# A two-layer hybrid backbone: softmax attention in two batches a group, retention scores by head pairs

## The chip, the cores and the metric

The kernel runs on one core of one Trainium2 chip. The metric is the device time of one execution in microseconds; what is shown is the median of the runs. The profile is that of one execution.

## The reference

Two post-norm layers act on 384 tokens of width 1024: 128 context tokens (block 0) and 256 latent tokens (blocks 1 and 2). All arithmetic is float32. A layer is a token mixer followed by a squared-ReLU MLP; both are modulated by a conditioning vector, and each ends in a layer norm. What matters here is the mixer:

```
p = h @ w_in                      # columns: q/kv latents, B's q k v g, C's q k v, D's q k v, four gates
A: latent attention, 4 heads      # dense; latent tokens also see 128 cached keys
B: retention, 4 heads             # (q k^T * decay) v, from both ends, plus a carried state
C: windowed attention, 4 q heads on 2 kv heads, a sink logit per head
D: dense attention, 4 q heads on 2 kv heads, q and k RMS-normalised
softmax: m = max(s); e = exp(s - m); p = e / sum(e) (+ exp(sink - m) for C)
retention_out: per head (o - mean) * rsqrt(var + eps) * gain * silu(gate)
y = sum_i sigmoid(gate_i) * (o_i @ w_branch_i); y = y @ w_o
x = layernorm(alpha * x + g1 * y);  f = square(relu(h @ w_up)) @ w_down;  x = layernorm(alpha * x + g2 * f)
```

Context tokens attend to the 128 context keys alone; a latent block attends to 256 latent keys and 128 cached ones, so its scores are 384 wide and those of the context block 128.

## The kernel before, in words

Every large product is made of three matmuls (`mm3`, L119 to L122): both operands are split into a high and a low float32r part, and high*high, low*high and high*low are added up in one PSUM bank. Each weight tile is loaded by a queue of SP, its high part is cast by ScalarE (L281) and its low part subtracted by VectorE (L125, `split_low`). `Stream` (L238) keeps four loads and two splits ahead.

The mixer of a layer goes in two stretches. First the input projection: chunks of 256 columns (L1068), each for the three token blocks `t` in turn (`proj`, L613): 8 steps of k, three matmuls each with 256 columns moving, into a bank of `psg`, then ScalarE moves it to a `t2` tile `tm[key, t]` (L588). Keys are "a", "c", "d", "b1" (the retention's q and k) and "b2" (its v and g). Layer 0 makes "c" and "a" beforehand; layer 1 has two chunks more. Then the four branches' gates and products (L1127), in the order A, C, D, B: `gates` (L1083) makes two gate tiles of 24 matmuls with 384 columns, `products` (L1094) multiplies the branch's output with its weights in two `psa` banks, and VectorE and GpSimd add them up (L1111 to L1117).

Between these groups of matmuls, `tick` (L461) calls `Pipe.step` (L425): it starts one more task of a list written by hand (L1037 to L1065) and calls the next stage of each task under way, oldest first. `held` keeps the instructions of a step behind what had been issued two steps before (`HOLD`); beyond that, the framework orders instructions of an engine by readiness and order of writing. After 22 ticks each tick also issues two or three steps of `ada_vector` (L346): VectorE operations over 1024 columns that make the modulation vectors of later stages (L370). These, and the scratch they write, share `t2` with the rest. Ahead of the last branch the list is run dry (L1131), the attention's memory is given back, and that of the second half (`p2`) is taken.

A task of softmax attention (`attend`, L621) is one group `g` (two heads `j`) and one token block `u`. Its stages are `scores` (L630: two banks of `psa`, one matmul for each head, mask, maximum, exponential with its sum on ScalarE, reciprocal and scaling on VectorE), `turn` (L665: transposes of p into two `psm` banks, copied to `pT` by ScalarE for j = 0 and by VectorE for j = 1) and `values` (L678). There are six of them for each branch, in the order u = 1, 2, 0 for each group. The retention's tasks are `prep_b` (L898: four transposes of q and k for each block), `states_b` (L909; its decayed k is made by GpSimd, L915), `scores_bp` (L937), `scores_b` (L948, one for each head) and `out_b` (L973). In C, D and B a head has 64 channels, so that the two heads of a pair lie in the lower and upper 64 partitions.

`out_product` (L1255) is the product that ends each half of a layer. Its last four steps of k are made block by block, with the layer norm of one block beside the matmuls of the next: `raw` (L1175), `stats` (L1185), `normalise` (L1194), `turn` (L1202), `high` and `low` into `hT`, and `update` on GpSimd. In the first half, the products of the first three MLP tiles run in between (`first_up`, L1415), with `square_u` (L1386) and `turn_u` (L1392); their squares are taken by VectorE (L1389), those of the other tiles by ScalarE (L1437). At the end of layer 1, the last block's second half is made in two pieces of 256 columns (L1308), and `end` (L1243) writes the result.

Pools that matter: `t2` has 12 tiles of 128x512 (`T2N`), `p` and `pT` two each (`PN`), `psa` three banks, `psm` and `psg` two, `pso` one.

Of the kernel before, what the change touches and what calls it, by code (L numbers as in the profile page):

```python
# [28 lines left out]
T2N = 12  # L29
# [64 lines left out]
def kernel(ctx, tc, a):  # L94
# [360 lines left out]
    for l in range(L):  # L455
# [165 lines left out]
        def attend(i, q_of, k_of, v_of, scale, sink=None, mask=None):  # L621
            ob = {}

            def batch(g, u):
                nb = 3 if u else 1
                nk = nb * P
                keys = slice(P, 512) if u else slice(0, P)
                st_ = {}

                def scores():  # L630
                    mx, neg, su = small([P, 2], "mx"), small([P, 2], "neg"), small([P, 2], "su")
# [7 lines left out]
                    for j in range(2):  # L639
                        s = ss[j]  # L640
                        if mask is not None and u:
                            c0 = P if u == 1 else 0
                            nc.vector.tensor_tensor(out=s[:, c0:c0 + P], in0=s[:, c0:c0 + P], in1=mask[u - 1], op=ALU.add)
                        nc.vector.reduce_max(mx[:, j:j + 1], s[:, :nk], axis=AX.X)
                    if sink is not None:
                        sk = sink[:, 2 * g:2 * g + 2]
                        nc.vector.scalar_tensor_tensor(out=mx, in0=mx, scalar=scale, in1=sk, op0=ALU.mult, op1=ALU.max)
                        nc.vector.tensor_scalar(out=neg, in0=mx, scalar1=-1.0, scalar2=None, op0=ALU.mult)
                        es = small([P, 2], "es")
# [3 lines left out]
                    for j in range(2):  # L653
                        nc.scalar.activation(p[:, j, :nk], ss[j][:, :nk], AF.Exp, bias=neg[:, j:j + 1], scale=scale,
                                             accum_out=su[:, j:j + 1])
# [4 lines left out]
                    for j in range(2):  # L660
                        nc.vector.tensor_scalar(out=p[:, j, :nk], in0=p[:, j, :nk], scalar1=su[:, j:j + 1], scalar2=None,
                                                op0=ALU.mult)
                    st_["p"] = p

                def turn():  # L665
                    p = st_["p"]
                    pT = at.tile([P, 2, NTOK], F32, tag="pT", name=nm("pT"), bufs=PN)
                    for j in range(2):
                        tb = bank(psm)
                        for b in range(nb):  # L670
                            nc.tensor.transpose(tb[:, b * P:(b + 1) * P], p[:, j, b * P:(b + 1) * P], ident)
                        if j == 0:
                            nc.scalar.copy(pT[:, j, :nk], tb[:, :nk])
                        else:
                            nc.vector.tensor_copy(pT[:, j, :nk], tb[:, :nk])
                    st_["pT"] = pT

                def values():  # L678
                    pT = st_["pT"]
                    if u == 1:  # L680
                        ob[g] = bank(pso)
                    if u == 1 and g == 0:
                        new_o(i)
                    for b in range(nb):
                        blk = b + 1 if u else 0
                        for j in range(2):
                            mm(ob[g][64 * j:64 * j + 64, u * P:(u + 1) * P], lhsT=v_of(g, j, blk),
                               rhs=pT[:, j, b * P:(b + 1) * P], start=(b == 0), stop=(b == nb - 1))
                    if u == 0:
# [7 lines left out]
            return [batch(g, u) for g in range(2) for u in (1, 2, 0)]  # L697
# [85 lines left out]
        def keys_a():  # L783
            for i in range(2):
                kb = bank(psa)
                for j in range(2):
                    h = 2 * i + j
                    mm(kb[64 * j:64 * j + 64, :], lhsT=w_uk[:, h * 64:(h + 1) * 64], rhs=ckvT, start=True, stop=True)
# [109 lines left out]
        def prep_b(t):  # L898
            def turn():
                if t == 0:  # L900
                    bt["qk"] = at.tile([P, 4, NTOK], F32, tag="k6", name=nm("qkB"), bufs=2)
                x = tm["b1", t]
                tb = bank(psm)
                for i in range(4):
                    nc.tensor.transpose(tb[:, i * P:(i + 1) * P], x[:, i * P:(i + 1) * P], ident)
                nc.scalar.copy(bt["qk"][:, :, t * P:(t + 1) * P], tb.rearrange("p (i n) -> p i n", i=4))
            return (turn,)

        def states_b():  # L909
            kds = []  # L910

            def dec():
                for d in range(2):
                    kd = t2("kd")
                    nc.gpsimd.tensor_tensor(  # L915
                        out=kd[:, 0:256].rearrange("p (h d) -> p h d", h=4),
                        in0=tm["b1", 0][:, 256:512].rearrange("p (h d) -> p h d", h=4),
                        in1=bt["dcol"][:, 4 + d].unsqueeze(2).to_broadcast([P, 4, 64]), op=ALU.mult)
                    kds.append(kd)

# [16 lines left out]
        def scores_bp():  # L937
            qk, dtab = bt["qk"], bt["dtab"]
            attp = bt["attp"] = t2("attp").rearrange("p (h n) -> p h n", h=4)
            for j in range(2):  # L940
                r = slice(64 * j, 64 * j + 64)
                pb = bank(psa)
                for i in range(2):
                    mm(pb[:, i * P:(i + 1) * P], lhsT=qk[r, 2 + i, 0:P], rhs=qk[r, i, 0:P], start=True, stop=True)
                nc.vector.tensor_tensor(out=attp[:, j::2], in0=pb[:, 0:256].rearrange("p (i n) -> p i n", i=2),
                                        in1=dtab[:, j::2, 1], op=ALU.mult)

        def scores_b(h):  # L948
            def f():
                qk, dtab = bt["qk"], bt["dtab"]  # L950
                i, j = divmod(h, 2)
                r = slice(64 * j, 64 * j + 64)
                pb = bank(psa)
                att = bt["att", h] = t2("atts").rearrange("p (b n) -> p b n", b=2)
                for jb in range(2):
                    mm(pb[:, jb * 256:(jb + 1) * 256], lhsT=qk[r, 2 + i, (1 + jb) * P:(2 + jb) * P], rhs=qk[r, i, P:NTOK],
                       start=True, stop=True)
                for jb in range(2):
                    nc.vector.tensor_tensor(
                        out=att[:, jb], in0=pb[:, jb * 256:(jb + 1) * 256],  # L960
                        in1=dtab[:, h, 1 - jb:3 - jb].rearrange("p a n -> p (a n)"), op=ALU.mult)
# [95 lines left out]
        for t in range(3):  # L1057
            pipe.add(*prep_b(t))
        pipe.add(*states_b())
        pipe.add(scores_bp)  # L1060
        for h in range(4):
            pipe.add(*scores_b(h))
# [5 lines left out]
        chunks = [("d", 0, None), ("d", 256, None), ("b1", 0, None), ("b1", 256, 0.125), ("b2", 0, None), ("b2", 256, 0.5)]  # L1068
# [577 lines left out]
```

## Time and profile before

| | |
|---|---|
| median of 3 runs | 1299.65 us (1298.49 to 1302.27) |
| the profiled execution | 1298.03 us |
| its span, first to last instruction | 1296.2 us |
| matmul instructions | 7362 |
| TensorE busy | 1269.4 us |
| mean granted TensorE clock | 0.996 of full speed |

The span is cut into stretches by the work that is done in them: the start with the first inputs up to 54.5 us; the mixer of layer 0 to about 345 us and its end and first layer norm to 402 us; the MLP to 680 us, with the second layer norm at its end; the mixer of layer 1 to about 975 us; its MLP to the end. A float32 matmul or score stands in the profile as two instructions, a transpose as one. Start times of neighbouring matmuls tell what each costs TensorE; their durations overlap.

### The profile page before, as it was taken

The numbers are of one execution on the slowest core, as the hardware profiler recorded it, in microseconds if no ns is written. First come the engines' busy times: TensorE is split into PE (matmuls) and PEld (weight loads), VectorE is DVE, ScalarE is ACT, GpSimd is POOL, SyncE is SP. The second block draws the span as 40 slices with busy tenths as digits, with TensorE's granted clock in tenths as the row PEclk, the third lists the DMA queues.
The fourth block names the chain that finished last, engine by engine and source line by source line (L and its number), as shares of the span: only waits on it lengthen the run. The fifth ranks groups of instructions, "written<-read, shape, count | busy, mean of one in ns | idle before, by whom it ended". The sixth has DMA issues, their size and how long they took to land. (4 is left out here: it accounts for less than half of the span.)

```text
span 1296.2 us, 19421 instructions
## 1 busy us (share of the span) xinstructions
PE 1269.4 (98%) x7362; PEld 1142.7 (88%) x7362; DVE 877.9 (68%) x1629; ACT 566.9 (44%) x1031; POOL 199.0 (15%) x218
## 2 busy tenths in 40 slices
PE   8999999999999999999999999999999999999996
PEld 6788888999988999999898888899998899999995
DVE  4655899996669999543485689967455993333336
ACT  4554445323535444444365445423343644444441
POOL 0010301323223000000061120012321500000003
PEclk9999999999999999999999999999999999999999
DMA  9833254665535888554323224543644263334421
GB/s 369 305 106 97 99 172 157 208 228 210 179 114 188 264 271 275 172 166 147 114 75 120 91 90 163 190 169 117 227 157 152 91 219 130 130 130 151 164 76 49
DMA packets 64686, 211.68 MB, mean 163 GB/s; under 512 B 9233, under 2 KB 13265, under 8 KB 64465
## 3 DMA queue, kind: packets, MB, share of 16 engines
q1 hardware_dynamic: 61872, 201.49, 45.1%
q0 software_dynamic: 2432, 8.42, 1.9%
q8 instruction: 58, 0.95, 0.3%
q10 hardware_dynamic: 288, 0.52, 0.1%
q14 instruction: 36, 0.29, 0.1%
HBM read 206.28 MB, written 4.13 MB: 162 GB/s over the span
## 5 line engine op out<-in xcount | busy, mean ns | idle before, releaser
L125 DVE TENSOR_TENSOR wl<-raw,wh 128x1024 fp32r<-128x1024 f32 x250 | 318.5, 1278 | 286.2 <-ACT wh L281 278.4
L281 ACT CAST wh<-raw 128x1024 fp32r<-128x1024 f32 x250 | 261.7, 1051 | 455.0 <-PE bank L121 297.4
L120 PE MATMUL bank<-hTh,wh 128*128 128x384 f32 x976 | 330.2, 338 | 0.3
L122 PE MATMUL bank<-hTh,wl 128*128 128x384 f32 x976 | 327.5, 336 | 0.0
L121 PE MATMUL bank<-hTl,wh 128*128 128x384 f32 x976 | 327.3, 335 | 0.0
L120 PEld LDWEIGHTS bank<-hTh,wh 128*128 128x128 f32 x976 | 183.3, 188 | 7.3 <-issue 2.9
L121 PEld LDWEIGHTS bank<-hTl,wh 128*128 128x128 f32 x976 | 183.3, 188 | 2.4 <-issue 0.3
L122 PEld LDWEIGHTS bank<-hTh,wl 128*128 128x128 f32 x976 | 183.2, 188 | 0.6 <-issue 0.3
L121 PE MATMUL bank<-wl,uh 128*128 128x512 f32 (+1 forms) x388 | 151.1, 389 | 0.0
L122 PE MATMUL bank<-wh,ul 128*128 128x512 f32 (+1 forms) x388 | 150.9, 390 | 0.0
L120 PE MATMUL bank<-wh,uh 128*128 128x512 f32 (+1 forms) x388 | 150.3, 387 | 0.0
L370 DVE CUSTOM_DVE_ANT_0 acc<-raw,csr,bT 128x1024 bf16<-128x1024 f32 x80 | 103.7, 1320 | 0.0
L120 PE MATMUL bank<-wh,hTh 128*128 128x256 f32 x336 | 99.9, 297 | 2.3 <-ACT tmc L594 2.3
L370 DVE CUSTOM_DVE_ANT_0 acc<-lnc,csr,bT 128x1024 bf16<-128x1024 f32 x80 | 99.6, 1280 | 0.0
L1117 POOL TENSOR_TENSOR tt<-tt,tt 128x384 f32<-128x384 f32 x48 | 61.6, 1303 | 240.6 <-DVE tt L1116 234.0
L121 PE MATMUL bank<-wl,hTh 128*128 128x256 f32 x336 | 95.4, 284 | 0.0
L122 PE MATMUL bank<-wh,hTl 128*128 128x256 f32 x336 | 95.4, 284 | 0.0
L122 PEld LDWEIGHTS bank<-wh,ul 128*128 128x128 f32 x388 | 72.8, 188 | 14.9
L121 PEld LDWEIGHTS bank<-wl,uh 128*128 128x128 f32 x388 | 72.8, 188 | 13.8
L120 PEld LDWEIGHTS bank<-wh,uh 128*128 128x128 f32 x388 | 72.9, 188 | 13.6
L120 PEld LDWEIGHTS bank<-wh,hTh 128*128 128x128 f32 x336 | 64.0, 190 | 6.3 <-ACT tmc L594 2.6
L121 PEld LDWEIGHTS bank<-wl,hTh 128*128 128x128 f32 x336 | 64.2, 191 | 2.5 <-issue 1.6
(263 smaller groups left out, 1810.2 us busy)
## 6 DMA issues: line engine op xcount, KB each, us to landing
raw<-in_w_g_dram SPq DMA_DIRECT2D x64, 512.0 KB, 3.7
raw<-in_w_d_dram SPq DMA_DIRECT2D x64, 512.0 KB, 3.5
raw<-in_w_u_dram SPq DMA_DIRECT2D x58, 512.0 KB, 3.8
raw<-in_w_av_dram SPq DMA_DIRECT2D x40, 512.0 KB, 3.4
lnc<-in_w_av_dram SPq DMA_DIRECT2D x40, 512.0 KB, 4.4
raw<-in_w_q_dram SPq DMA_DIRECT2D x28, 512.0 KB, 4.6
raw<-in_w_ada_dram SPq DMA_DIRECT2D x16, 512.0 KB, 8.5
raw<-in_w_b_dram SPq DMA_DIRECT2D x16, 512.0 KB, 3.7
```

The source lines that it names most:

```text
L120: mm(out, lhsT=a_hl[0], rhs=b_hl[0], start=start, stop=False)
L121: mm(out, lhsT=a_hl[0], rhs=b_hl[1], start=False, stop=False)
L122: mm(out, lhsT=a_hl[1], rhs=b_hl[0], start=False, stop=stop)
L125: nc.vector.tensor_tensor(out=low, in0=x, in1=high.bitcast(F32), op=ALU.subtract)
L281: nc.scalar.copy(wh, raw)
L370: nc.vector.tensor_tensor_reduce(out=alloc().bitcast(BF16), in0=w, in1=csr[:, c], scale=1.0, scalar=bT[:, l, u, b:b + 1], op0=ALU.mult, op ...
L1117: nc.gpsimd.tensor_tensor(out=acc[c], in0=acc[c], in1=t_, op=ALU.add)
```

## The change

- `Pipe.step` calls the stages of one step in two rounds: first all that are not marked late, then those marked late. Late are the transposes of the softmax (`turn`) and the new first stage of `states_b`.
- `attend` makes two tasks of a group in place of three: blocks 1 and 0 together (384 and 128 columns side by side in one bank for each head), and block 2. The score matmuls of the two heads stand next to each other for each block. `p` and `pT` are 512 wide. The group's output is moved after block 2.
- The retention's q and k are no longer projected by token and then transposed: the chunks "b1" become "qk", made by channels (`qk_b`: weights stationary, 384 tokens moving), four groups of 24 matmuls in place of six, each with one tick. `prep_b` goes. `states_b` transposes k of block 0 back (two transposes), and VectorE, not GpSimd, multiplies it with the decay. The new tile has a tag of its own ("kb").
- `scores_b` takes two heads at once, with their matmuls next to each other in two banks; `scores_bp` likewise.
- `keys_a` makes one matmul of 128 columns in place of two of 64.
- In the layer norm ScalarE normalises the last block's second half too, and the last block of all is no longer cut into pieces of 256 columns. `square_u` squares on ScalarE.
- `T2N` is 10 in place of 12, and the scratch for dynamic DMA 4096 in place of 8192.

```diff
     def step(self):
...
-            for t in list(self.live):
-                if t:
-                    with held(marks):
-                        t.pop(0)()
-                if not t:
-                    self.live.remove(t)
+            stages = [t.pop(0) for t in self.live if t]
+            for late in (False, True):
+                for f in stages:
+                    if getattr(f, "late", False) == late:
+                        with held(marks):
+                            f()
+            self.live = [t for t in self.live if t]
...
                 def scores():
...
-                    p = at.tile([P, 2, NTOK], F32, tag="p", name=nm("p"), bufs=PN)
-                    ss = []
-                    for j in range(2):
-                        s = bank(psa)
-                        mm(s[:, :nk], lhsT=q_of(g, j, slice(u * P, (u + 1) * P)), rhs=k_of(g, j, keys),
-                           start=True, stop=True)
-                        ss.append(s)
+                    p = at.tile([P, 2, 512], F32, tag="p", name=nm("p"), bufs=PN)
+                    ss = [bank(psa) for _ in range(2)]
+                    for u, nb, c in segs:
+                        for j in range(2):
+                            mm(ss[j][:, c], lhsT=q_of(g, j, slice(u * P, (u + 1) * P)),
+                               rhs=k_of(g, j, slice(P, 512) if u else slice(0, P)), start=True, stop=True)
...
+                turn.late = True
...
-            return [batch(g, u) for g in range(2) for u in (1, 2, 0)]
+            return [batch(g, us) for g in range(2) for us in ((1, 0), (2,))]
...
-        def prep_b(t):
...
+        def qk_b(i0, scale):
+
+            def f(w, i):
+                if i0 + i == 0:
+                    bt["qk"] = at.tile([P, 4, NTOK], F32, tag="kb", name=nm("qkB"))
+                b = bank(psg)
+                for k in range(KT):
+                    mm3(b[:, :NTOK], tuple(q[:, i * P:(i + 1) * P] for q in w[k]), hk(k), k == 0, k == KT - 1)
+                if scale is None:
+                    nc.scalar.copy(bt["qk"][:, i0 + i, :], b[:, :NTOK])
+                else:
+                    nc.scalar.mul(bt["qk"][:, i0 + i, :], b[:, :NTOK], scale)
+            return f
...
             def dec():
+                tb = bank(psm)
+                for i in range(2):
+                    nc.tensor.transpose(tb[:, i * P:(i + 1) * P], bt["qk"][:, 2 + i, 0:P], ident)
                 for d in range(2):
                     kd = t2("kd")
-                    nc.gpsimd.tensor_tensor(
+                    nc.vector.tensor_tensor(
...
-        def scores_b(h):
+        def scores_b(i):
+
             def f():
                 qk, dtab = bt["qk"], bt["dtab"]
...
+                pbs = [bank(psa) for _ in range(2)]
                 for jb in range(2):
...
+                    for j in range(2):
+                        r = slice(64 * j, 64 * j + 64)
+                        mm(pbs[j][:, jb * 256:(jb + 1) * 256], lhsT=qk[r, 2 + i, (1 + jb) * P:(2 + jb) * P],
+                           rhs=qk[r, i, P:NTOK], start=True, stop=True)
...
-        chunks = [("d", 0, None), ("d", 256, None), ("b1", 0, None), ("b1", 256, 0.125), ("b2", 0, None), ("b2", 256, 0.5)]
+        chunks = [("d", 0, None), ("d", 256, None), ("qk", 0, None), ("qk", 2, 0.125), ("b2", 0, None), ("b2", 256, 0.5)]
...
             def normalise():
                 for h in range(2):
-                    if t == 2 and h == 1:
-                        nc.vector.tensor_scalar(out=z[h], in0=src[h], scalar1=mv[:, 0:1], scalar2=rs[:, 1:2],
-                                                op0=ALU.subtract, op1=ALU.mult)
-                    else:
-                        nc.scalar.activation(z[h], src[h], AF.Identity, bias=rs[:, 3:4], scale=rs[:, 1:2])
+                    nc.scalar.activation(z[h], src[h], AF.Identity, bias=rs[:, 3:4], scale=rs[:, 1:2])
...
-                    cuts = (0, 512, 768, 1024)
-                    last_part(2, None, cuts)
-                    sums(2, None, cuts)
+                    last_part(2)
+                    sums(2)
...
-            nc.vector.tensor_tensor(out=r, in0=r, in1=r, op=ALU.mult)
+            nc.scalar.activation(r, r, AF.Square)
```

## Rows read from the trace of the kernel before

**Rows 1.** The page's first part: busy time and instructions of each engine.

```profile
PE 1269.4 (98%) x7362; PEld 1142.7 (88%) x7362; DVE 877.9 (68%) x1629; ACT 566.9 (44%) x1031; POOL 199.0 (15%) x218
```

**Rows 2.** Busy time by stretch: its length, then PE, PEld, DVE, ACT, POOL (instructions).

```profile
80.00:330.00 250.00, 245.95 (x1601) 223.84 (x1600) 205.68 (x463) 104.32 (x231) 50.61 (x46) 1.00 0.49 163
...
205.00:285.00 80.00, 79.90 (x483) 73.01 (x483) 79.38 (x133) 29.20 (x56) 21.69 (x15) 1.00 0.63 206
...
820.00:960.00 140.00, 140.00 (x837) 135.34 (x837) 92.85 (x183) 47.85 (x78) 31.45 (x30) 1.00 0.48 169
```

**Rows 3.** What TensorE waited for: us in total, times, longest.

```profile
PE bank L671 <- DVE p L661: 3.1, 5, 1.2
PE bank L1395 <- DVE r L1389: 2.3, 4, 0.7
PE bank L120 <- ACT tmc L594: 2.3, 1, 2.3
...
PE bank L1027 <- DVE oB L1019: 1.9, 1, 1.9
```

**Rows 4.** Timeline of TensorE (start, us): first and last of nine 256-column, eight 384-column matmuls.

```profile
60.80 0.28 PE L120 MATMUL bank<-wh,hTh 128*128 128x256 f32 x1
...
61.76 0.28 PE L122 MATMUL bank<-wh,hTl 128*128 128x256 f32 x1
...
215.01 0.33 PE L120 MATMUL bank<-hTh,wh 128*128 128x384 f32 x1
...
216.23 0.33 PE L121 MATMUL bank<-hTl,wh 128*128 128x384 f32 x1
```

**Rows 5.** The same: the retention's transposes of one block, and the matmul behind them.

```profile
233.52 0.60 PE L905 MATMUL bank<-ident,tmb 128*128 128x128 f32 x4
233.87 0.42 PE L121 MATMUL bank<-hTl,wh 128*128 128x384 f32 x1
```

**Rows 6.** The same: the retention's scores of one head, and the matmul behind them.

```profile
261.53 1.13 PE L956 MATMUL bank<-qkB 64*128 64x256 f32 x4
262.59 0.44 PE L120 MATMUL bank<-o,wh 128*128 128x384 f32 x1
```

**Rows 7.** The same: scores of two heads next to each other, and of one alone.

```profile
128.82 0.92 PE L636 MATMUL bank<-qk 64*128 64x384 f32 x4
...
163.99 0.91 PE L636 MATMUL bank<-qk 64*128 64x384 f32 x2
```

**Rows 8.** The same: values of a context block by themselves, and the matmul behind them.

```profile
117.58 0.44 PE L687 MATMUL bank<-pT,va 128*64 128x128 f32 x4
117.95 0.38 PE L120 MATMUL bank<-wh,hTh 128*128 128x256 f32 x1
```

**Rows 9.** Squares of 128x384 on VectorE and ScalarE, normalising on ScalarE: groups of the span.

```profile
L1389 DVE TENSOR_TENSOR r<-r 128x384 f32<-128x384 f32 x6 | 7.7, 1287 | 0.0
...
L1437 ACT ACTIVATE r<-r 128x384 f32<-128x384 f32 x58 | 30.5, 526 | 1.7
...
L1200 ACT ACTIVATE z<-z,lnrs 128x512 f32<-128x512 f32 x15 | 11.6, 811 | 26.9 <-POOL lnrs L1192 26.9
```

**Rows 10.** Timeline of VectorE at the end: two 512-column operations, the first and last 256-column ones.

```profile
1280.55 0.70 DVE L1179 SCALAR_TENSOR_TENSOR bank<-x,bank 128x512 f32<-128x512 f32 x1
...
1281.28 0.70 DVE L1182 BATCH_NORM_STATS2 lnst<-bank 128x6 f32<-128x512 f32 x1
...
1285.40 0.43 DVE L1178 TENSOR_TENSOR bank<-bank,lnc 128x256 f32<-128x256 f32 x1 [0.65 <-PE bank L122]
...
1288.27 0.26 DVE L1186 BATCH_NORM_AGGREGATE lnmv<-lnst 128x2 f32<-128x24 f32 x1
```

**Rows 11.** Groups of VectorE in the stretch of 205 to 285 us.

```profile
L370 DVE CUSTOM_DVE_ANT_0 acc<-raw,csr,bT 128x1024 bf16<-128x1024 f32 x33 | 44.0, 1365 | 0.0
```

**Rows 12.** Groups of VectorE in the span: copies of transposed p, and decay on 256 columns.

```profile
L675 DVE COPY pT<-bank 128x384 f32<-128x384 f32 x24 | 13.3, 555 | 8.4 <-PE bank L671 8.4
...
L945 DVE TENSOR_TENSOR attp<-bank,dtab 128x256 f32<-128x256 f32 x4 | 1.5, 412 | 0.0
```

More of the change, by code (lines that the diff above doesn't have):

```diff
@@ L28 @@
 T1N = 11
-T2N = 12
+T2N = 10
 PN = 2
@@ new lines, in scores @@
+                    for i, (u, nb, c) in enumerate(segs):
+                        for j in range(2):
+                            s = ss[j][:, c]
+                            if mask is not None and u:
+                                c0 = P if u == 1 else 0
+                                nc.vector.tensor_tensor(out=s[:, c0:c0 + P], in0=s[:, c0:c0 + P], in1=mask[u - 1],
+                                                        op=ALU.add)
+                            nc.vector.reduce_max(mx[:, i, j:j + 1], s, axis=AX.X)
@@ L785, in keys_a @@
                 kb = bank(psa)
-                for j in range(2):
-                    h = 2 * i + j
-                    mm(kb[64 * j:64 * j + 64, :], lhsT=w_uk[:, h * 64:(h + 1) * 64], rhs=ckvT, start=True, stop=True)
+                mm(kb, lhsT=w_uk[:, i * P:(i + 1) * P], rhs=ckvT, start=True, stop=True)
                 nc.scalar.copy(kTA[0:64, 2 * i, :], kb[0:64, :])
@@ L949, in f @@
             def f():
                 qk, dtab = bt["qk"], bt["dtab"]
[L951 to L954, printed above, removed]
+                pbs = [bank(psa) for _ in range(2)]
                 for jb in range(2):
-                    mm(pb[:, jb * 256:(jb + 1) * 256], lhsT=qk[r, 2 + i, (1 + jb) * P:(2 + jb) * P], rhs=qk[r, i, P:NTOK],
-                       start=True, stop=True)
@@ L958, in f @@
[L958 to L961, printed above, removed]
+                    for j in range(2):
+                        r = slice(64 * j, 64 * j + 64)
+                        mm(pbs[j][:, jb * 256:(jb + 1) * 256], lhsT=qk[r, 2 + i, (1 + jb) * P:(2 + jb) * P],
+                           rhs=qk[r, i, P:NTOK], start=True, stop=True)
@@ L1056 @@
             pipe.add(*b)
-        for t in range(3):
-            pipe.add(*prep_b(t))
         pipe.add(*states_b())
         pipe.add(scores_bp)
-        for h in range(4):
-            pipe.add(*scores_b(h))
+        for i in range(2):
+            pipe.add(*scores_b(i))
         for t in (1, 2, 0):
@@ L1076 @@
         for key, c0, scale in chunks:
-            proj(by_k([stream.next(), stream.next()], 4), 256, evac_to(key, c0, scale), tick)
+            w = by_k([stream.next(), stream.next()], 4)
+            if key == "qk":
+                for i in range(2):
+                    qk_b(c0, scale)(w, i)
+                    tick()
+            else:
+                proj(w, 256, evac_to(key, c0, scale), tick)
         acc = [None] * KT
@@ L1165, in layer_norm @@
             gb, lg_, lb_ = consts[cnd], consts[2], consts[3]
-            width = 256 if mod is None and t == 2 else 512
-            st = p2.tile([P, 4, 6], F32, tag="lnst", name=nm("lnst"), bufs=2)
+            st = p2.tile([P, 2, 6], F32, tag="lnst", name=nm("lnst"), bufs=2)
             mv = p2.tile([P, 2], F32, tag="lnmv", name=nm("lnmv"), bufs=2)
@@ L1180, in raw @@
                                                op0=ALU.mult, op1=ALU.add)
-                for i in range(c.start, c.stop, width):
-                    nc.vector.bn_stats(st[:, len(groups)], src[h][:, i:i + width])
-                    groups.append(i)
+                nc.vector.bn_stats(st[:, h], src[h][:, c])
             def stats():
-                nc.vector.bn_aggr(mv, st[:, 0:len(groups)])
+                nc.vector.bn_aggr(mv, st)
                 nc.vector.tensor_scalar(out=rs[:, 0:1], in0=mv[:, 1:2], scalar1=EPS, scalar2=None, op0=ALU.add)
```

93 lines of the change are left out of this document (45 added, 48 removed).

## The prediction

> **What bounds the kernel now.** I read the busy times first: TensorE is busy for 1269.4 of 1296.2 us, VectorE for 68%, ScalarE 44%, GpSimd 15% [rows 1]. A busy TensorE may still be stretched, so next come the stretches: in layer 0's mixer it is busy for 245.95 of 250 us, and over 205 to 285 us for 79.90 of 80 [rows 2]. What it waits for by name is little: 3.1 us for the scaled p ahead of the softmax's transposes, 2.3 us for squares, 2.3 us for an evacuation at the start of the projection, 1.9 us for the last retention output [rows 3]. So the span is the sum of what TensorE is given to do, and an instruction less on it, or a pause less between two kinds of its work, is time gained, as long as the other engines keep up. Whether they do is the second thing to see: over 205 to 285 us VectorE is busy for 79.38 of 80 us [rows 2], 44.0 of them in operations for later modulation vectors [rows 11]. Two engines are full at once there. In the mixer of layer 1 VectorE has room: 92.85 of 140 us over 820 to 960 [rows 2].
>
> The sum goes by start times. Nine matmuls of 256 columns start over 0.96 us, so one takes 0.120; eight of 384 start over 1.22 us, so one takes 0.174 [rows 4].
>
> **The change, part by part.** Terms are for both layers; minus is time gained.
>
> q and k by channels: a layer's 144 matmuls of 0.120 us (17.3 us) become 96 of 0.174 (16.7): -0.6, twice, **-1.2 us**. Columns are the same; only the fixed part of a matmul falls away. The new evacuation by ScalarE is hidden by its idle 56% [rows 1]; if ScalarE were late, the two `psg` banks would hold up the next group.
>
> No transposes of q and k: six visits (three blocks, two layers) of 0.35 us, from 233.52 to 233.87, and the matmul behind each is 0.42 long, not 0.33: 0.09 more of restart [rows 4, 5]. 6 x 0.44 = 2.6. Added are two visits with half as many transposes, 0.18 + 0.09 each: 0.5. **-2.1 us**. The decayed k moves to VectorE: four operations on 256 columns of 0.412 [rows 12], 1.6 us, hidden unless VectorE is full; then it counts in the last term.
>
> Retention scores: a head takes 1.06 us (261.53 to 262.59) and a restart of 0.10 (0.44 against 0.34) [rows 6]. That two heads side by side cost what one costs shows in the softmax's scores: four instructions for two heads 0.92 us, two for one head alone 0.91 [rows 7]. Eight visits become four of the same length: 4 x 1.16, **-4.6 us**. Bounds: 0 if the heads aren't issued in pairs and the visits stay, 4.6 if all are.
>
> Softmax heads of C and D: most pairs are already side by side, but I find three pairs of 384 columns and two of 128 issued apart in the trace, one of them at 163.99 us [rows 7]. Written next to each other, they would save some 0.94 and 0.5 each, 3.9 in all; nothing forces it, since readiness orders them, and more pairs could also come apart. Between +3.9 and -3.9, and nearer to the gain, since both banks are now taken first: half of it, **-1.9 us**.
>
> 36 batches become 24: twelve times a context block's scores and values join those of another block. Values by themselves take 0.37 us and a restart of 0.10 (0.38 against 0.28) [rows 4, 8]. Sure is only the restart, 24 x 0.10, **-2.4 us**; above, 24 x 0.37 = 8.9; below 0.
>
> Transposes last: the p they read has a score visit more of time. Of the 3.1 us of waits [rows 3] I take half: **-1.5 us**. Late next would be the copies of the transposed p, see the rivals.
>
> The list is run dry ahead of the last branch. In layer 0 there are 18 + 24 ticks and 42 tasks, the last of four stages, so three steps run with no matmul group between them; the 1.9 us wait for the retention output [rows 3] is there. Now 31 tasks meet 16 + 24 ticks: **-1.9 us**.
>
> Squares of the first tiles: VectorE takes 1287 ns for each, ScalarE 526 for the same shape [rows 9], and TensorE waited 2.3 us for them [rows 3]: **-2.3 us**; below, 0 if ScalarE is busy there. The Trainium skill ("ScalarE: Activation LUTs", Rules for kernel authors) says the opposite for this operation: multiply on VectorE, not on ScalarE; by that rule the sum would lack these 2.3 us. Here the rows disagree with it, and I go by them; what speaks for it is a rival.
>
> Normalising on ScalarE (0.811 us [rows 9]) stands one behind the other there, and VectorE is free earlier to give back the bank that the next transposes want: taken as 0, between +0.8 and -0.8 for each of three norms.
>
> The end: VectorE starts the last two pieces at 1285.40, when TensorE has left the bank, so the finer cut lets nothing start earlier; six operations take until 1288.27, 2.87 us. Three of 512 columns, 0.73 apart, take 2.19 [rows 10]: **-0.7 us**.
>
> `keys_a`: two halves that ran side by side become one: 0. `T2N` 10: three tiles fewer are wanted from it (b1), two fewer are there. Early in layer 0, though, a, c and d are all resident, and an evacuation may wait for a tile; cover is the two banks of `psg`. 0, with the one such wait as the upper bound, 2.3 us [rows 3], in each layer. The smaller DMA scratch is used by GpSimd's own loads; its idle 85% [rows 1] covers a wait there: 0.
>
> These make -18.6 us. Against them, VectorE in layer 0: less time for the same modulation steps, which now start two gate groups later (tick 23 of 40, not of 45) while it was full already. Layer 0's share of what is gained in the mixer is about half of 2.1 + 4.6 + 2.4 + 1.9 + 1.5, and its 1.9, so 8.2 us; between none and all of this comes back as waits for VectorE. I take **+3.0**, less than half, since the last branch has no pipe work and lets it catch up. Sum: -15.6 us.
>
> The profiled execution took 1298.0 us, 1.6 less than the median of 1299.65; it gives 1282.4, the median 1284.0. I predict **1284**.
>
> **The rivals.**
> - VectorE takes over in layer 0. For it: 79.38 of 80 us [rows 2]. Against it: 44.0 of these [rows 11] are for later use, with some slack. All 8.2 us come back, leaving 10.4: 1289.
> - The pairs don't come about. Two banks of three must be free at once, and `products` wants the same ones; single heads in the trace [rows 7] show that it happens. Lost are 4 x 1.06 of the retention and the 1.9: 1290. The Trainium skill warns of this in its own way ("TensorEngine Tiling (Array Packing)", Gotcha 1: PSUM Pressure): row tiles write to different banks, so tiling takes more PSUM; no row here shows a price for it.
> - The squares gain nothing: ScalarE's queue also holds the casts and the normalising, 0.811 us each [rows 9], ahead of them, and TensorE waits for ScalarE as it did for VectorE. The 2.3 us are lost: 1286. The rule named above would have it so.
> - Slower: the late transposes make the copies of pT late. They now stand behind the next batch's scores on TensorE (0.92 us [rows 7]) and its softmax on VectorE, are wider (0.73 for 512 columns [rows 10], not 0.555 [rows 12]), and the next step begins with the values that read them. Where a step is short or VectorE full, a batch would wait up to 1.6 us. With 16 of the 24 batches (C and D) that is 26 us: 1310. It decides from 1.0 us a batch. Against it: a whole group of 24 matmuls lies between the two, 2.9 to 4.2 us [rows 4], and VectorE idles 8.4 us ahead of these copies now [rows 12], so they needn't queue.
>
> **How the numbers follow.** My forecast gets 0.52, VectorE 0.17, no pairs 0.10, the squares 0.04, late copies 0.12; 0.05 for the gains and losses nearly cancelling. What a measurement can tell from no change is about 0.3%, 3.9 us, so the first four lie on the faster side except for their edges. Faster 0.82, same 0.07, slower 0.11. The range: below, all of the softmax pairs (-2.0 more), half of the wider bound for joined visits (-3.2), the other half of the waits (-1.5) and VectorE at nothing (-3.0) come to 1274, and a little for order that I can't foresee: 1272. Above it takes in both of the first rivals together, at most 1295 (18.6 - 8.2 - 6.1 are gained), and a wait for `t2`, to 1298. The late copies stay outside.
>
> **What would show it.** Right: the retention's scores in visits of eight instructions in about 1.06 us, TensorE's wait for squares gone, the wait for oB gone in layer 0, 136 fewer instructions on TensorE (96 of the projection, 20 transposes, 8 of `keys_a`, 12 at the end) but a busy share that stays at 98%, and the last block's operations after TensorE's end 0.7 us shorter. Wrong: visits of four instructions as now; VectorE full into the last branch of layer 0 with TensorE waiting for banks that it holds (first rival); waits of `values` for pT (third). The forecast is wrong if layer 1's mixer isn't at least 5 us shorter, since nothing there is full.

## The result and the profile after

The changed kernel takes **1293.64 us** (median of 5 runs, 1291.69 to 1294.39) against 1300.70 (1298.49 to 1302.27) of the kernel before on the same chip: ratio **0.9945 [0.993, 0.996]**, 7.1 us less, where 15.6 were forecast; the time lies inside the range of the prediction, 1272 to 1298. The profiled execution took 1292.02 us; its span is 1290.3.

The page's busy line of the changed kernel, against [rows 1]:

```profile
PE 1258.5 (98%) x7226; PEld 1139.1 (88%) x7226; DVE 865.3 (67%) x1572; ACT 567.0 (44%) x1014; POOL 198.9 (15%) x214
```

TensorE has 136 instructions less, as forecast, and is busy for 10.9 us less. But the span is only 5.9 us shorter: TensorE idles for 31.8 us now and for 26.8 before. Where, the timeline of TensorE tells by its landmarks: the first projection matmul and the first matmul of w_o, in layer 0 and layer 1. Kernel before (start, duration in us):

```profile
55.81 0.39 PE L120 MATMUL bank<-wh,hTh 128*128 128x256 f32 x1 [2.30 <-ACT tmc L594]
...
350.37 0.39 PE L120 MATMUL bank<-wh,mh 128*128 128x512 f32 x1
...
672.06 0.27 PE L120 MATMUL bank<-wh,hTh 128*128 128x256 f32 x1
...
980.11 0.39 PE L120 MATMUL bank<-wh,mh 128*128 128x512 f32 x1
```

The same four of the changed kernel:

```profile
55.51 0.39 PE L120 MATMUL bank<-wh,hTh 128*128 128x256 f32 x1 [2.30 <-ACT tmc L597]
...
352.97 0.39 PE L120 MATMUL bank<-wh,mh 128*128 128x512 f32 x1
...
672.76 0.27 PE L120 MATMUL bank<-wh,hTh 128*128 128x256 f32 x1
...
976.85 0.39 PE L120 MATMUL bank<-wh,mh 128*128 128x512 f32 x1
```

Layer 0's mixer, from the first of these to the second, grew from 294.6 to 297.5 us; layer 1's shrank from 308.1 to 304.1. The rest gained: from the first w_o matmul to the first of the down projection 2.0 us in each layer (55.9 to 53.9), more than the 2.3 that were forecast for the squares in both together, and 0.7 at the end, as forecast. So the gain is missing in layer 0's mixer. What TensorE waited for, from the view of its waits in the changed kernel (whole span; us in total, times, longest), against [rows 3]:

```profile
PE bank L122 <- DVE wl L125: 7.1, 5, 3.0
...
PE bank L772 <- DVE rsa L747: 1.5, 1, 1.5
...
PE bank L1049 <- DVE oB L1041: 0.9, 2, 0.5
...
PE bank L681 <- DVE p L671: 0.5, 2, 0.2
```

The wait for squares (2.3 us) is gone and that for the scaled p fell from 3.1 to 0.5. New is the first line: TensorE waits for `wl`, the low half of a weight tile, which VectorE makes by a subtraction. Four of these five waits, 6.5 us, lie in layer 0, at 270, 277, 302 and 306 us; the longest, in the timeline of TensorE:

```profile
276.65 0.44 PE L122 MATMUL bank<-hTh,wl 128*128 128x384 f32 x1 [3.05 <-DVE wl L125]
```

Busy time by stretch of the changed kernel (PE, PEld, DVE, ACT, POOL, then PEclk, DMA share, GB/s), against [rows 2], and two stretches more:

```profile
80.00:330.00 250.00, 240.46 (x1533) 220.23 (x1532) 202.25 (x439) 101.36 (x217) 50.88 (x44) 0.99 0.47 162
205.00:285.00 80.00, 72.90 (x443) 68.12 (x440) 76.59 (x162) 22.58 (x37) 25.04 (x17) 0.98 0.54 182
820.00:960.00 140.00, 138.26 (x810) 135.81 (x809) 103.50 (x186) 45.84 (x68) 35.05 (x30) 1.00 0.54 188
185.00:205.00 20.00, 20.00 (x139) 17.67 (x139) 13.51 (x30) 10.00 (x26) 0.00 (x0) 1.00 0.23 81
225.00:305.00 80.00, 71.54 (x409) 68.24 (x408) 80.00 (x162) 22.42 (x34) 27.33 (x19) 0.98 0.59 198
```

VectorE is busy for 80.00 of 80 us over 225 to 305, and TensorE for 71.54. But right ahead of that, over 185 to 205, VectorE is busy for 13.51 of 20 us and the DMA share is 0.23. An engine that is too slow for its work doesn't idle just before it is overrun. The modulation steps (L370) tell what is missing there: counted in two stretches of the changed kernel, 170 to 182 and 208 to 282 us (duration min/median/max in ns, starts of the first and the last):

```profile
L370 DVE CUSTOM_DVE_ANT_0 acc<-raw,csr,bT x6: 1271/1274/1284, 170.9 to 181.0; 128x1024 bf16<-128x1024 f32 x6
...
L370 DVE CUSTOM_DVE_ANT_0 acc<-raw,csr,bT x30: 1252/1275/1744, 208.1 to 279.3; 128x1024 bf16<-128x1024 f32 x30
```

After the step at 181 us none starts for 27 us; the kernel before ran eight between 185.5 and 207.7. The 42 that are left then fall behind 208 us, the last at 303.9, on top of the last branches' work. The timeline of VectorE in the gap shows it idling and no step starting:

```profile
180.96 1.27 DVE L370 CUSTOM_DVE_ANT_0 acc<-raw,csr,bT 128x1024 bf16<-128x1024 f32 x1
...
189.50 1.23 DVE L125 TENSOR_TENSOR wl<-raw,wh 128x1024 fp32r<-128x1024 f32 x1 [1.76 <-ACT wh L281]
...
194.60 0.18 DVE L668 RECIPROCAL su<-su 128x4 f32<-128x4 f32 x1 [2.00 <-ACT p L663]
...
205.79 1.23 DVE L125 TENSOR_TENSOR wl<-raw,wh 128x1024 fp32r<-128x1024 f32 x1 [1.91 <-ACT wh L281]
...
208.13 1.27 DVE L370 CUSTOM_DVE_ANT_0 acc<-raw,csr,bT 128x1024 bf16<-128x1024 f32 x1
```

### The profile page after: what moved, and what is told of

Same layout as the page of the kernel before. It is cut to its first block, busy times and chain, and to the rows that moved or that the text cites. A ratio compares the mean times of both kernels' runs of the same rounds, so it can differ in the third digit from the quotient of the medians.

```text
span 1290.3 us, 19064 instructions
## 1 busy us (share of the span) xinstructions
PE 1258.5 (98%) x7226; PEld 1139.1 (88%) x7226; DVE 865.3 (67%) x1572; ACT 567.0 (44%) x1014; POOL 198.9 (15%) x214
## 5 line engine op out<-in xcount | busy, mean ns | idle before, releaser
L125 DVE TENSOR_TENSOR wl<-raw,wh 128x1024 fp32r<-128x1024 f32 x250 | 320.8, 1289 | 295.9 <-ACT wh L281 295.6
L122 PE MATMUL bank<-hTh,wl 128*128 128x384 f32 x1040 | 350.0, 337 | 5.7 <-DVE wl L125 5.7
L120 PE MATMUL bank<-hTh,wh 128*128 128x384 f32 x1040 | 351.8, 338 | 0.6 <-ACT tt L1116 0.6
L121 PE MATMUL bank<-hTl,wh 128*128 128x384 f32 x1040 | 349.0, 336 | 0.0
L121 PE MATMUL bank<-wl,uh 128*128 128x512 f32 x384 | 150.4, 392 | 0.0
L122 PE MATMUL bank<-wh,ul 128*128 128x512 f32 x384 | 150.3, 392 | 0.0
L120 PE MATMUL bank<-wh,uh 128*128 128x512 f32 x384 | 149.7, 390 | 0.0
L370 DVE CUSTOM_DVE_ANT_0 acc<-raw,csr,bT 128x1024 bf16<-128x1024 f32 x80 | 103.6, 1321 | 0.0
L370 DVE CUSTOM_DVE_ANT_0 acc<-lnc,csr,bT 128x1024 bf16<-128x1024 f32 x80 | 100.5, 1292 | 0.0
L120 PE MATMUL bank<-wh,hTh 128*128 128x256 f32 x240 | 72.2, 301 | 2.3 <-ACT tmc L597 2.3
L121 PE MATMUL bank<-wl,hTh 128*128 128x256 f32 x240 | 69.4, 289 | 0.0
L122 PE MATMUL bank<-wh,hTl 128*128 128x256 f32 x240 | 68.7, 286 | 0.0
L663 ACT ACTIVATE p<-bank,neg 128x384 f32<-128x384 f32 (+1 forms) x72 | 35.9, 509 | 33.7 <-DVE neg L660 19.5
```

The lines of the kernel that those rows point to most:

```text
L120: mm(out, lhsT=a_hl[0], rhs=b_hl[0], start=start, stop=False)
L121: mm(out, lhsT=a_hl[0], rhs=b_hl[1], start=False, stop=False)
L122: mm(out, lhsT=a_hl[1], rhs=b_hl[0], start=False, stop=stop)
L125: nc.vector.tensor_tensor(out=low, in0=x, in1=high.bitcast(F32), op=ALU.subtract)
L370: nc.vector.tensor_tensor_reduce(out=alloc().bitcast(BF16), in0=w, in1=csr[:, c], scale=1.0, scalar=bT[:, l, u, b:b + 1], op0=ALU.mult, op ...
L663: nc.scalar.activation(p[:, j, c], ss[j][:, c], AF.Exp, bias=neg[:, i, j:j + 1], scale=scale, accum_out=su[:, i, j:j + 1])
```

## The experiments

**Theory (tiles).** A modulation step's output `acc` is a `t2` tile. With ten of them the tiles are all held by branch work from 181 to 208 us, the steps stand still, and VectorE has to make up for them later, when it is full. **Rival (ticks).** The steps simply start too late, since the list now begins them two gate groups nearer to the end (`TICKS_FROM`), and VectorE is short of time whatever tiles there are.

More `t2` tiles in the changed kernel weren't tried, and which tiles hold the pool full isn't read from the trace. But `acc` can go into another buffer that is idle there, and that tests whether a place for `acc` is what is missing.

The experiments ran on three chips, each beside the kernel before on the same chip; so every ratio is to that one. Where the interval of a ratio overlaps that of the run it is compared with, the text says so.

**A tile of its own.** From here on "own tile" means this edit of the changed kernel:

```
-        ada_v = ada_vector(AV_GATES[l], lambda: t2("acc"))
+        ada_v = ada_vector(AV_GATES[l], lambda: at.tile([P, 4, 256], F32, tag="va",
+                           name=nm("acc")).rearrange("p a n -> p (a n)")[:, :512])
```

> The changed kernel, but the scratch that the modulation steps write lies where branch A's values lay (free by then) and no longer in one of the ten t2 tiles. Theory TILES (the steps stop between 181 and 208 us of layer 0 because no t2 tile is free, and are crowded into the time after, ahead of the weight splits): steps run through that gap, TensorE's 7.1 us of waits for wl (L125) fall below 2.5, and the time falls by 4 to 8 us against the changed kernel, to 1286 to 1290. Theory TICKS (the steps start two gate groups later, since 16 ticks in place of 18 go to the projection): their first step stays at 171 us, and less than 2 us are gained. Theory LOAD (VectorE simply has more work than fits before the last branch): less than 2 us gained, waits for wl stay above 5 us.

Measured: **1282.65 us**, ratio to the kernel before 0.9868 [0.9853, 0.9883]: 11 us better than the changed kernel, more than expected. TensorE's waits in it, those left out being 2.1 us or less and the same as in the changed kernel:

```profile
PE bank L120 <- ACT tmc L597: 2.3, 1, 2.3
...
PE bank L120 <- DVE atts L981: 1.6, 2, 1.4
...
PE bank L681 <- DVE p L671: 1.0, 3, 0.4
PE bank L699 <- DVE pT L685: 0.7, 1, 0.7
```

There is none for `wl`. The steps in the 26 us from 182 to 208, and busy time by stretch:

```profile
L370 DVE CUSTOM_DVE_ANT_0 acc<-raw,csr,bT x7: 1264/1279/1285, 186.3 to 203.9; 128x1024 bf16<-128x1024 f32 x7
```

```profile
80.00:330.00 250.00, 247.88 (x1597) 230.00 (x1596) 212.79 (x449) 107.47 (x226) 54.90 (x46) 1.00 0.51 169
185.00:205.00 20.00, 19.65 (x146) 17.27 (x145) 19.93 (x42) 9.96 (x22) 0.00 (x0) 1.00 0.49 150
205.00:285.00 80.00, 78.57 (x482) 75.59 (x481) 77.62 (x161) 23.25 (x39) 27.81 (x19) 1.00 0.59 187
```

Seven steps fill the gap, VectorE is busy for 19.93 of 20 us there, and TensorE has 247.88 us of the 250 instead of 240.46. The instructions are the same, only one buffer is another. Layer 0's mixer takes 285.1 us (55.60 to 340.65), 9.5 less than before the change.

**The other side: does the old kernel lack tiles too?** The same edit in the kernel before.

> The kernel before with the same edit as e1: the modulation steps' scratch out of its twelve t2 tiles. If the shortage of tiles is the changed kernel's alone (ten tiles): no change beyond 2 us, 1298 to 1302, since its steps already run evenly from 154 to 281 us. If twelve were too few as well: 3 us or more faster.

Measured: 1303.42 us, ratio 1.0017 [1.0008, 1.0026]: no gain, and some 2 us slower, which isn't explained. With twelve `t2` tiles the steps of that kernel had no shortage; it is the changed kernel's alone. That twelve would be enough in the changed kernel too isn't shown by this.

**Only layer 0.** `lambda: t2("acc") if l else` the own tile.

> e1 with the own scratch tile in layer 0 alone. In layer 1 of e1 the stretch from the first gate to the output product was 2.1 us longer than in the changed kernel, the projection 1.4 shorter. If the tile matters only where VectorE is full: within 1.5 us of e1, 1281 to 1284. If layer 1's share counts too: 2 us or more slower than e1.

Measured: **1281.35 us**, 0.9861 [0.9837, 0.9886]. All of the gain sits in layer 0. It can't be told from the own tile in both layers, and both beat the two kernels of this case.

**Earlier steps in the changed kernel** (rival):

```
-TICKS_FROM = 22
+TICKS_FROM = 20
```

> The changed kernel with TICKS_FROM 20 in place of 22: the modulation steps start at the same gate group of layer 0 as in the kernel before. Theory TICKS: waits for wl fall below 2.5 us, 4 to 8 us gained, 1286 to 1290. Theory TILES: the steps that start earlier still stop when the tiles run out; half or less of it is gained, 1 to 4 us, 1290 to 1293. Theory LOAD: under 2 us.

Measured: 1293.16 us, 0.9945 [0.9932, 0.9957], the changed kernel's own ratio. TensorE still waits for `wl`:

```profile
PE bank L122 <- DVE wl L125: 4.3, 3, 2.4
```

An earlier start doesn't give back the time, while another buffer does: the rival falls. The trace agrees: the steps now start at 156.1 us, but stop all the same, between the ones at 196.2 and 209.1.

**The start of the steps, with their own tile**, at 20, 16 and 24 instead of 22.

> Both edits: own scratch tile and TICKS_FROM 20. Theories TILES and TICKS: at least what the better of the two gains, 5 to 9 us, 1285 to 1289, with waits for wl below 1.5 us. Theory LOAD: under 2 us, and VectorE full to the end of the third branch.

> Own scratch tile and TICKS_FROM 16: the steps start with the first gate group of layer 0 and, in layer 1, six ticks earlier, beside the softmax of C. If room on VectorE is all that counts, as good as or better than TICKS_FROM 20 (1284 to 1288); if the softmax of C is then late (VectorE was busy for 42.9 of 47 us over 138 to 185 in the changed kernel), TensorE waits there instead and 1 to 4 us are lost against it.

> e1 with TICKS_FROM 24: the steps start one gate group later. From 16, 20 and 22 ticks came 1289.1, 1287.0 and 1282.7, so starting later was better as long as the softmax of C is under way. If that goes on: 1279 to 1282. If the steps then no longer fit before the last branch of layer 0: 2 to 6 us slower than e1, with waits for the weight splits (L125) at the end of the third branch.

Measured: 1287.01 us, 0.9895 [0.9881, 0.9908]; 1289.12, 0.9915 [0.9901, 0.9928]; 1287.67, 0.9897 [0.9882, 0.9912]. All three are 4 to 6.5 us slower than with 22 (with 20 and 24 the intervals just overlap). With 20 TensorE waits more for p and again for `wl`, as if the steps stood in the way of the branches' own VectorE work. With 16 the late softmax of C that was expected doesn't show as a wait for p (0.7 us in all), and the loss stays open. With 24 two waits come at the end of layer 0's mixer and just behind it, for `wl` at 313 and for tt at 350 us; the last step starts at 313.0 there, and at 301.5 with 22. The waits with 20 and then with 24:

```profile
PE bank L681 <- DVE p L671: 2.5, 4, 1.3
...
PE bank L122 <- DVE wl L125: 2.1, 2, 1.1
```

```profile
PE bank L120 <- DVE tt L1142: 2.0, 1, 2.0
PE bank L122 <- DVE wl L125: 1.8, 1, 1.8
```

**Joining the batches**, undone on top of the own tile:

```
-            return [batch(g, us) for g in range(2) for us in ((1, 0), (2,))]
+            return [batch(g, us) for g in range(2) for us in ((1,), (0,), (2,))]
```

> e1 with three batches a group again (blocks 1, 0, 2 in this order): 37 tasks in a layer in place of 31, all else as in e1. Predicted for joining them were 2.4 us, at least 0 and at most 8.9: 1284 to 1288 if that holds, with some 0.4 us more for each of the twelve visits that come apart. If fewer tasks count through the ticks left over for the modulation steps more than through the visits, more than 4 us are lost, 1287 to 1292, with waits for VectorE in layer 0's gates.

Measured: **1299.26 us** (10 runs), 0.9985 [0.9971, 1.0]: 16.6 us worse, far outside what was expected, and nearly all that the change gains with the own tile. Its busy line and the larger waits:

```profile
PE 1266.4 (97%) x7226; PEld 1141.5 (88%) x7226; DVE 867.1 (67%) x1620; ACT 569.3 (44%) x1030; POOL 201.0 (15%) x214
```

```profile
PE bank L120 <- DVE atts L981: 4.6, 2, 3.2
PE bank L681 <- DVE p L671: 3.9, 5, 1.8
...
PE bank L120 <- ACT tt L1116: 1.8, 1, 1.8
...
PE bank L120 <- ACT p L663: 1.0, 1, 1.0
```

In these two profiles the spans differ by 20.3 us (1278.7 and 1299.0), more than the medians do. The same 7226 instructions keep TensorE busy for 9.7 us more (1256.7 against 1266.4), and it idles for 10.6 more (32.6 against 22.0). Most of the idling is named above: `atts` 3.0 us more, p 2.9, tt 1.8, p by ScalarE 1.0; another 1.7 is a wait for `rsa`, which comes and goes between runs (see the last experiment).

The longer busy time is mostly the clock. The mean granted clock is 0.990 in this profile and 0.997 with the own tile; over some 1,290 us that makes about 9 us, an estimate. Here are the longest wait in the timeline of TensorE, and four stretches in the view by stretch, at the lower of the two levels; the own tile's profile has 1.00 over the same four:

```profile
872.62 0.44 PE L120 MATMUL bank<-o,wh 128*128 128x384 f32 x1 [3.22 <-DVE atts L981]
```

```profile
58.30:61.70 3.40, 3.40 (x18) 3.40 (x17) 3.35 (x12) 1.10 (x3) 1.10 (x2) 0.50 0.41 100
304.00:307.40 3.40, 3.40 (x13) 3.40 (x12) 3.40 (x7) 0.00 (x0) 3.40 (x3) 0.50 0.75 233
761.40:764.80 3.40, 3.40 (x18) 2.85 (x18) 1.92 (x5) 1.85 (x6) 0.11 (x1) 0.50 0.00 0
874.00:877.40 3.40, 3.40 (x12) 3.40 (x11) 3.37 (x5) 0.84 (x1) 3.40 (x3) 0.51 0.34 130
```

The last three stand shortly behind waits, for tt (until 302.44), p (until 759.85) and `atts` (until 872.62). TensorE is busy throughout them and does about half the work, so each costs some 1.7 us more, an estimate from these rows. The first follows a wait that the own tile's profile has too, so it isn't put down to the edit.

Why the waits grow isn't shown. Half as many batches again are half as many chains again of maximum, exponential, sum and scaling, 48 instructions more on VectorE and 16 on ScalarE; but VectorE's busy time is only 2.8 us longer (864.3 to 867.1). The list is also six tasks longer in each layer, and what stands behind the batches comes later: the retention's first score visit at 256.80 and 860.88 us in the two layers, with the own tile at 219.16 and 813.91. No run keeps one of these and undoes the other.

```profile
256.80 1.13 PE L975 MATMUL bank<-qkB 64*128 64x256 f32 x8
```

The run undoes the joining alone, with the late transposes, the smaller pool and the new list around it; so 16.6 is its worth in the changed kernel with the own tile, and not what it would bring to the one before.

**The late round**, undone on top of the own tile (`if getattr(f, "late", False) == late:` becomes `if not late:`, so that the transposes stand where they are written).

> e1 (changed kernel with the scratch in its own tile) without the late round: the stages of a step run oldest first, as in the kernel before. If putting the transposes last is worth its 1.5 us as predicted: 1283 to 1286, with more wait of the softmax's transposes for p (L681 on L671) than e1's 1.0 us. If it is worth nothing: within 1 us of e1's 1282.65. If late transposes cost (the third rival): 1278 to 1281.

Measured: 1285.69 us, 0.9886 [0.9866, 0.9905], some 3 us worse. The interval overlaps that of the own tile; against the next experiment, run on the same chip, it is 3.3 us. But not by the wait that it was meant for: p costs 1.1 us here and 1.0 there. What grew is the wait for `atts` (1.6 to 3.0), and `rsa` is there with 1.3. The profile doesn't settle how the late round helps, or whether it does.

**The order within a pair.** Retention scores by head, then block, as two single heads would issue them, on top of the own tile:

```
-                for jb in range(2):
-                    for j in range(2):
+                for j in range(2):
+                    for jb in range(2):
```

> e1 with the retention's score matmuls of a pair written head by head in place of alternating: four visits of eight instructions as before, other order, nothing else. If two heads cost what one does only when they alternate: each visit goes from 1.06 to 2.12 us, 4 x 1.06 = 4.2 us in all, 1286 to 1288. If the gain came from having four visits in place of eight: within 1 us of e1, 1282 to 1284.

Measured: 1282.38 us, 0.9863 [0.9844, 0.9881], no difference. A visit takes as long in both orders; the timeline of TensorE with the own tile, and with this order:

```profile
219.16 1.13 PE L975 MATMUL bank<-qkB 64*128 64x256 f32 x8
220.22 0.44 PE L120 MATMUL bank<-hTh,wh 128*128 128x384 f32 x1
```

```profile
220.83 1.14 PE L975 MATMUL bank<-qkB 64*128 64x256 f32 x8
221.90 0.44 PE L120 MATMUL bank<-hTh,wh 128*128 128x384 f32 x1
```

Eight instructions in 1.06 and 1.07 us, where four took 1.06 [rows 6]. What counts is that both heads are in one visit, not that they alternate.

**Squares back on VectorE**, on top of the own tile (line 1407: `nc.vector.tensor_tensor(out=r, in0=r, in1=r, op=ALU.mult)`).

> e1 with the six squares of the first MLP tiles back on VectorE. Predicted was 2.3 us for them over both layers; the stretch of the first layer norm became 2.0 us shorter in each layer. If the squares are all of that: 1286 to 1287.5 and both stretches 2.0 us longer (53.9 to 55.9). If they are 2.3 of it: 1284 to 1286.

Measured: 1285.05 us, 0.9876 [0.9851, 0.99]. The stretch from w_o to the down projection takes 54.7 us in both layers (with the own tile 53.95), so the squares give 0.8 in each, not all of the 2.0 that the change gained there. The median is 2.4 us above the own tile's, but the two intervals overlap almost wholly. VectorE takes 911 ns for a square here, not the 1287 of [rows 9].

**Half of the last block's normalising back on VectorE**, on top of the own tile.

```
-                    nc.scalar.activation(z[h], src[h], AF.Identity, bias=rs[:, 3:4], scale=rs[:, 1:2])
+                    if t == 2 and h == 1:
+                        nc.vector.tensor_scalar(out=z[h], in0=src[h], scalar1=mv[:, 0:1], scalar2=rs[:, 1:2],
+                                                op0=ALU.subtract, op1=ALU.mult)
+                    else:
+                        nc.scalar.activation(z[h], src[h], AF.Identity, bias=rs[:, 3:4], scale=rs[:, 1:2])
```

> e1 with the last block's second half normalised on VectorE again. Predicted was 0 for it, between +0.8 and -0.8 for each of three norms. If it is the other part of the 2.0 us by which each first layer norm became shorter: 1283.5 to 1286; if it is nothing: within 1 us of e1.

Measured: 1286.49 us, 0.9888 [0.9873, 0.9903]; the interval overlaps the own tile's. And the two stretches that hold the edited operations stand at 53.9 us as with the own tile; the profile's difference lies in layer 1's projections, behind a wait that the edit doesn't touch:

```profile
PE bank L772 <- DVE rsa L747: 2.3, 1, 2.3
```

That wait, for branch A's norms at the start of layer 1's mixer, is 1.5 us in the changed kernel, 1.2 to 1.7 in seven other runs, and 0.1 or none in the own tile and two more, though no edit touches it. The granted clock falls to 0.50 right behind it, from 669.9 to 673.3 us, some 1.7 us more; the two are about the 3.8 us by which the spans of the profiles differ. So where it was moved, the normalising costs nothing either way; why the wait arises stays open, and the slower median with it. With neither edit giving it alone, 1.2 of each 2.0 us after w_o is open: either is enough for most of it, or it is another part.

## Why the prediction was right and wrong

The direction was right. That TensorE's list is the span, as long as the other engines keep up, holds in part: the condition failed in layer 0, and there the gain went. With the steps in their own tile the measured gain is 17.3 us (1299.92 to 1282.65), and the sum of the gains was 18.6. That the two are close is luck: without the joined batches, all the other parts and the own tile together are at a ratio of 0.9985, and what joining gives, with the same number of instructions, lies in waits and clock.

**The step that failed is "`T2N` 10: three tiles fewer are wanted from it (b1), two fewer are there", costed at 0 with an upper bound of one wait of 2.3 us in each layer.** A place for `acc` outside the ten tiles brings back 11 us, all in layer 0. I counted the tiles that the branches hold and not a user that starts on its own time: the modulation steps, whose `acc` comes from the same pool. And the bound was for the wrong thing. The wait isn't TensorE's, it is an idle VectorE; TensorE pays 60 to 100 us after the gap, for `wl`, when 42 steps are left for the last 96 us.

**VectorE in layer 0, +3.0.** The first rival (all 8.2 us come back there, 1289) came nearest in place and time, but it gave the wrong cause: VectorE isn't too slow, it goes without steps for 27 us beforehand. Given tiles, layer 0's mixer gains 9.5 us, so little of what was gained there is taken back. Starting the steps two groups later, which I held against the change, does no harm: with the own tile 22 is the best of the four values run.

**Joined batches, -2.4, bound 8.9.** Far too small: 16.6. I costed TensorE's visits alone. About half of the difference between the two profiles sits in waits for other engines, and most of the rest in the clock, which fell behind three of these waits. Whether the chains of the softmax or the six tasks more cause the waits stays open.

**Parts don't add up.** Undone one at a time, joining (16.6), the late round (3.0) and squares (2.4) already make 22.0 of a gain of 17.3 by the medians, though the last two aren't clear of noise. Each is the price with all others in place; that what one leaves late is paid for again by the next would explain it, but isn't shown.

**Retention scores, -4.6.** Right in the amount per visit, four visits of 1.06 us and their restarts less; no run measures what that gives in time. The second rival (pairs don't come about) falls. Had the heads been issued one behind the other within a visit, even that would have cost nothing.

**Transposes last, -1.5.** Measured about 3.0, not clear of noise. The wait for p fell from 3.1 to 0.5 in the changed kernel, but the run without the late round shows it no larger, so the reason given is not borne out. The rival of late copies falls: the waits for pT come to 0.7 us.

**Squares, -2.3.** The wait is gone; with squares undone, the two stretches together are 1.6 longer. ScalarE takes 527 ns for each, as [rows 9] said. So the Trainium skill's rule ("ScalarE: Activation LUTs", Rules for kernel authors: multiply on VectorE) doesn't decide here, where VectorE takes 911 to 1287 ns; the figure beside the rule is for bf16, and these squares are float32. The rival built on it falls.

**Normalising, 0; the end, -0.7; q and k by channels, -1.2, and their transposes, -2.1.** The first is borne out where it stands, the second is 0.66 by the span less TensorE's end (10.88 to 10.22). The last two have no run of their own, and neither have the softmax pairs of C and D, -1.9. Of these the trace tells enough: in the changed kernel four pairs of 384 columns are still issued apart (first heads at 134.84, 179.2, 767.6 and 784.62 us), where there were three, and none of 128, where there were two. At 0.91 us more and twice 0.48 less that is about nothing. **The list run dry, -1.9:** the wait for oB is 0.9 us in the changed kernel and not among those of the own tile.

**What I said would show it wrong** was right to name: "VectorE full into the last branch of layer 0 with TensorE waiting" is what the trace shows, though TensorE waits for weight splits and not for banks, and layer 1's mixer is 4.0 us shorter, not 5. With the own tile it is 3.3 shorter, and 5.3 with it in layer 0 alone (by the same two starts, 660.91 and 963.62). VectorE isn't full there, but waits that the kernel before doesn't have stand in it: `rsa` 1.5, `atts` 0.8, `wl` 0.6 and oB 0.3 us in the changed kernel.

## What to carry to other kernels

Before a buffer pool is made smaller, list everything that takes a tile from it, with when each holds it; the users that nobody waits for (work for later) are the ones that stop silently. When an engine is full and something waits for it, look at the stretch ahead: an idle engine there means that its work was held back, and a place for the result can give back what a faster engine would not. A wait of TensorE can cost more than its length, when the clock falls behind it. A part's worth is found by taking it out of the finished kernel, and is not to be added to those of the others.

## What the hardware showed that I had not expected

- Two heads of retention scores, on different halves of TensorE's rows, share a visit of 1.06 us whether their instructions alternate or come one head after the other.
- TensorE's granted clock falls for a few us some time after it idled, and rises again, inside a run whose mean is 0.99. In the changed kernel it stands at 0.57 over 56 to 60 us, behind the 2.3 us wait, and again over 278 to 282, where TensorE had been busy for 4.43 us of the eight ahead; a 384-column matmul then lasts 0.52 us and the next starts 0.32 later, not 0.174. That is the lower of the two levels, 1.2 GHz. With the own tile the wait at 55.60 is the same (2.29 us) and the clock stays at 1.00 over 56 to 60. So a difference of 1 to 2 us between single profiles can be the clock alone, and isn't read as an effect by itself.

The changed kernel by stretch, and then with the own tile:

```profile
56.00:60.00 4.00, 4.00 (x24) 4.00 (x23) 3.95 (x13) 1.63 (x4) 1.11 (x2) 0.57 0.40 121
...
270.00:278.00 8.00, 4.43 (x24) 3.90 (x25) 8.00 (x15) 0.56 (x2) 0.78 (x1) 1.00 0.40 140
278.00:282.00 4.00, 4.00 (x16) 4.00 (x15) 4.00 (x8) 0.86 (x1) 0.00 (x0) 0.57 0.80 269
```

```profile
56.00:60.00 4.00, 4.00 (x36) 4.00 (x36) 3.95 (x13) 2.81 (x10) 1.10 (x2) 1.00 0.32 74
```
